# Four-tile dots, one more halving sum, a new order of gathers at the end and fewer address checks in a hard-max attention kernel

## The chip, the cores and the metric

One core of one Trainium2 chip. The metric is device time in microseconds (us) of one execution, lower is better, given as the median of several runs. A profile is one execution; its span is about 2 us shorter than the device time. PE is the matmul engine, PEld its weight loads, DVE the vector engine, ACT the scalar engine, POOL the engine that issues the gathers, SP the engine that issues most stores.

## The reference

```python
# q, k, v: (4, 4096, 128) float32
logits = np.matmul(q, k.transpose(0, 2, 1))
best = np.argmax(logits, axis=-1)
return v[b_idx, best, :].astype(np.float32)
```

Each query row gets the one value row whose key has the largest dot product with it.

## The kernel before

The 16384 query rows are 128 tiles of 128 rows. Keys are taken in groups of four. For each tile, PE computes combinations of the four keys' logits in 16 bits, ACT takes absolute values (A) and a rectified copy (E), and DVE folds everything into one score per group (`W`, line 260) and takes the best eight groups (`MAX8`, line 264). That is the main loop. Behind it runs a refinement: POOL gathers the three key differences of the best group (`kg`, "group gather"), DVE multiplies them with the query and sums (the "dots"), picks the winner (`win`), POOL gathers its value row (`vr`, "value gather") and SP stores it. Rows too close to call are flagged and done again exactly, for the first half of the tiles in mid-kernel and for the second half at the end; the end gathers their three key groups (`FK`), their queries (`FQ`) and their values (`FV`), and scatters the rows to the output.

The dots, in groups of `m` tiles (a generator; each `yield` lets the main loop go on):

```python
    def dots(c, x, m):
        ...
        for i in range(0, m, h):                       # h = min(m, 2)
            nc.vector.tensor_tensor(out=prod[:, i:i + h], in0=kg[...], in1=natq[...], op=OP.mult)
            yield gap
        nc.vector.tensor_tensor(out=p1, in0=prod[:, :, :, 0:64], in1=prod[:, :, :, 64:128], op=OP.add)
        yield gap
        nc.vector.tensor_tensor(out=p2, in0=p1[:, :, :, 0:32], in1=p1[:, :, :, 32:64], op=OP.add)
        yield "dve",
        nc.vector.tensor_reduce(out=d[:, x - c0:x - c0 + m, 1:4], in_=p2, axis=AX_X, op=OP.add)
```

What POOL issues in iteration `it`: first group gathers (`near_q`), then flagged-row gathers (`fast`), then as many value gathers (`late_q`) as the rate leaves room for:

```python
        while near_q and (n < 1 + behind or near_q[0] in marks):
            ...
        rate = 2.42 if it < 72 else 2.5 if it < 104 else 2.55 if it < 120 else 3.0
        room[0] = min(room[0] + rate - busy, 3.0) - n
        for i in range(2):
            if room[0] >= 1 and late_q:
                take_late(1)
                room[0] -= 1
```

The end, once DVE has the flagged keys' addresses `gb`:

```python
        late(LATE)                                     # 6 value gathers
        get(FK[:, 0, :], k_flat, gb[:, 0:1], B * Sk)
        get(FQ, q_flat, row, P * T)
        for r in (1, 2):
            get(FK[:, r, :], k_flat, gb[:, r:r + 1], B * Sk)
        ...
        late(1 << 20)                                  # all value gathers that are left
        ...
        get(FV, v_flat, win, B * Sk)                   # then the scatter
```

## Time and profile before

| | before |
|---|---|
| device time, median | 444.38 us (444.23 to 445.06, 4 runs) |
| span of the profiled run | 443.07 us |
| busy share of the span | PE 86%, DVE 92%, ACT 85%, POOL 70% |
| tiles 16 to 71 (stage A) | 164.40 us |
| tiles 72 to 107 (stage B) | 120.36 us |
| tiles 108 to the fold of tile 127 (stage C) | 61.11 us |
| fold of tile 127 to the final scatter | 29.88 us |

The stages are cut at the start of a tile's fold (DVE W). An engine's busy share is an average over stages with different limits.

### The profile page before, as it was taken

The numbers are of one execution on the slowest core, as the hardware profiler recorded it, in microseconds if no ns is written. First come the engines' busy times: TensorE is split into PE (matmuls) and PEld (weight loads), VectorE is DVE, ScalarE is ACT, GpSimd is POOL, SyncE is SP. The second block draws the span as 40 slices with busy tenths as digits, with TensorE's granted clock in tenths as the row PEclk, the third lists the DMA queues.
The fourth block names the chain that finished last, engine by engine and source line by source line (L and its number), as shares of the span: only waits on it lengthen the run. The fifth ranks groups of instructions, "written<-read, shape, count | busy, mean of one in ns | idle before, by whom it ended". The sixth has DMA issues, their size and how long they took to land.

```text
span 443.1 us, 6303 instructions
## 1 busy us (share of the span) xinstructions
PE 379.9 (86%) x1830; PEld 168.3 (38%) x1830; DVE 408.3 (92%) x770; ACT 377.0 (85%) x437; POOL 310.8 (70%) x335
## 2 busy tenths in 40 slices
PE   8999999999999999999998889899988999893010
PEld 4444444444444444444443333343333333331000
DVE  2688999999999999999999999999999999999861
ACT  2999999999999999999998889889988999983000
POOL 8423456777767887777778776777777777756773
PEclk9999999999999999999999999999999999998555
DMA  7944989473316999843346884354322333322341
GB/s 129 198 100 81 149 143 142 102 134 86 107 49 141 167 151 165 167 111 93 83 109 133 159 153 102 88 133 113 86 83 86 85 92 104 90 75 80 91 149 53
DMA packets 52869, 50.55 MB, mean 114 GB/s; under 512 B 34136, under 2 KB 40890, under 8 KB 52832
## 3 DMA queue, kind: packets, MB, share of 16 engines
q0 software_dynamic: 19072, 33.87, 39.0%
q1 hardware_dynamic: 33760, 16.26, 15.1%
q8 instruction: 14, 0.23, 0.2%
q14 instruction: 23, 0.19, 0.1%
HBM read 40.05 MB, written 14.55 MB: 123 GB/s over the span
## 4 chain that ended last, share of the span: by engine, by line
ACT 30%; issue 23%; DVE 17%; PE 11%; POOL 10%; DMA 7%; POOLq 0%; ACTq 0%; DVEq 0%; SPq 0%
ACT A L234 25%; DVE TOP L264 5%; POOL vr L341 5%; DVE W L260 5%; ACT E L247 5%; POOL kg L282 5%; PE psn L225 4%; DMA kg<-k,cand 4%; PE psn L244 3%; PE pd L225 3%; DVE prod L300 2%; DMA natk<-in_k_dram 2%; DVE p L305 1%; DMA FK<-in_k_dram,gb_e 1%; DMA vr<-in_v_dram,win_w 1%
## 5 line engine op out<-in xcount | busy, mean ns | idle before, releaser
L234 ACT ACTIVATE A<-pd 128x1024 f16<-128x1024 f32 x256 | 259.8, 1041 | 12.7 <-PE pd L225 11.6
L282 POOL DMA_INDIRECT kg<-k,cand x126 | 126.1, 1001 | 80.0 <-DVE cand L276 47.1
L260 DVE SCALAR_TENSOR_TENSOR W<-psn,E 128x1024 int16<-128x1024 f32 x128 | 168.0, 1312 | 7.4 <-ACT E L247 5.3
L225 PE MATMUL psn<-kT,qT 128*128 128x512 f16 x512 | 151.9, 378 | 12.7 <-ACT A L234 5.8
L225 PE MATMUL pd<-kT,qT 128*128 128x512 f16 x512 | 151.8, 378 | 9.6 <-ACT A L234 8.7
L341 POOL DMA_INDIRECT vr<-in_v_dram,win x126 | 130.8, 1038 | 39.5 <-issue 35.3
L264 DVE MAX8 TOP<-W 128x8 f32<-128x1024 f32 x128 | 157.9, 1234 | 0.0
L225 PEld LDWEIGHTS <-qT 128*128 128x128 f16 x1024 | 98.0, 97 | 154.8 <-issue 65.3
L244 PE MATMUL psn<-A,identh 128*128 128x512 f16 x512 | 152.1, 378 | 0.0
L247 ACT ACTIVATE E<-psn 128x1024 int16<-128x1024 f32 x128 | 132.2, 1033 | 3.6 <-PE psn L244 2.9
L244 PEld LDWEIGHTS <-identh 128*128 128x128 f16 x512 | 49.6, 97 | 60.8
L300 DVE TENSOR_TENSOR prod<-kg,natq 128x768 f16<-128x768 f16 x63 | 35.5, 563 | 4.5 <-DMA kg<-k,cand 4.4
L205 ACT ACTIVATE kT<-uk 128x256 f16<-128x256 f32 x48 | 20.1, 420 | 1.6 <-PE uk L202 1.6
L305 DVE TENSOR_TENSOR p<-prod 128x384 f16<-128x384 f16 (+1 forms) x45 | 19.7, 438 | 0.1
L310 DVE TENSOR_REDUCE D<-p 128x6 f32<-128x192 f16 (+1 forms) x45 | 19.1, 426 | 0.1
L201 PE MATMUL uk<-identh,natk 128*128 128x128 f16 x96 | 15.8, 218 | 0.0
L484 PE MATMUL fp_e<-n_e,tri 128*128 128x1 f32 x2 | 0.6, 362 | 16.6 <-DVE n_e L482 16.6
L308 DVE TENSOR_TENSOR p<-p 128x192 f16<-128x192 f16 (+1 forms) x45 | 13.3, 298 | 0.1
L202 PEld LDWEIGHTS <-natk 128*128 128x128 f16 x96 | 9.3, 97 | 7.0 <-issue 4.4
L66 POOL DMA_DIRECT2D natk<-in_k_dram x19 | 11.3, 601 | 0.8 <-POOLq L890 0.8
L201 PEld LDWEIGHTS <-natk 128*128 128x128 f16 x96 | 9.4, 98 | 5.6
L69 POOL DMA_DIRECT2D natq<-in_q_dram x15 | 9.1, 609 | 0.0
(152 smaller groups left out, 143.3 us busy)
## 6 DMA issues: line engine op xcount, KB each, us to landing
out_dram<-vr SPq DMA_DIRECT2D x31, 256.0 KB, 2.2
natq<-in_q_dram POOLq DMA_DIRECT2D x12, 256.0 KB, 5.2
natk<-in_k_dram POOLq DMA_DIRECT2D x10, 256.0 KB, 7.1
k<-kd SPq DMA_DIRECT2D x18, 128.0 KB, 3.4
k<-natk POOLq DMA_DIRECT2D x6, 384.0 KB, 8.3
kg<-k,cand POOLq DMA_INDIRECT x126, 3.0
vr<-in_v_dram,win POOLq DMA_INDIRECT x126, 2.6
natk<-in_k_dram POOLq DMA_DIRECT2D x8, 128.0 KB, 6.2
```

The lines of the kernel that those rows point to most:

```text
L201: nc.tensor.matmul(out=o, lhsT=natk[b % 2][:, h, 4 * m + x, :], rhs=identh, start=True, stop=False)
L205: nc.scalar.activation(out=kT[b % 2][:, c:c + 256], in_=ps, func=AF.Copy)
L225: nc.tensor.matmul(out=ps[:, n * 512:(n + 1) * 512], lhsT=qT[b % 2][:, qt * P:(qt + 1) * P], rhs=kT[b % 2][:, u * 1024 + n * 512:u * 1024 ...
L234: nc.scalar.activation(out=A, in_=ps, func=AF.Abs)
L244: nc.tensor.matmul(out=ps[:, n * 512:(n + 1) * 512], lhsT=identh, rhs=A[:, n * 512:(n + 1) * 512], start=False, stop=True)
L247: nc.scalar.activation(out=E, in_=ps, func=AF.Relu, scale=QSCALE)
L260: nc.vector.scalar_tensor_tensor(out=W_t[t % NW].bitcast(I16)[:, 1::2], in0=ps, scalar=QSCALE, in1=E, op0=OP.mult, op1=OP.max)
L264: nc.vector.max(out=TOP[:, t, :], in_=W_t[t % NW].bitcast(FP32))
L282: near_q.append(lambda j=j: nc.gpsimd.indirect_dma_start(out=kg[:, j].rearrange("p f d -> p (f d)"), out_offset=None, in_=k16[t0 // NQT], ...
L300: nc.vector.tensor_tensor(out=prod[:, i:i + h], in0=kg[:, i:i + h], in1=natq[b % 2][:, x + i - b * NQT:x + i + h - b * NQT, :].unsqueeze(2 ...
L305: nc.vector.tensor_tensor(out=p1, in0=prod[:, :, :, 0:64], in1=prod[:, :, :, 64:128], op=OP.add)
L341: late_q.append(lambda j=j: nc.gpsimd.indirect_dma_start(out=vr[:, j, :], out_offset=None, in_=v_flat, in_offset=IOA(ap=win[:, i + j:i + j ...
```

## The change

Its intent: less DVE work for the dots of tiles 72 to 107, a cheaper last reduce, group gathers that reach DVE in time, and an earlier start of the flagged rows at the end. The diff is whole; the line of `cuts` gives the same list as before.

```diff
-LATE = 6
+LATE = 4
@@ dots
         yield "dve",
+        if m == 4:
+            p3 = rp.tile([P, 4, 3, 16], FP16, tag="p3", name=f"p3_{x}")
+            nc.vector.tensor_tensor(out=p3, in0=p2[:, :, :, 0:16], in1=p2[:, :, :, 16:32], op=OP.add)
+            p2 = p3
+            yield "dve",
@@ put_values
+        edge = dict(bounds_check=B * Sk - 1, oob_is_err=False) if chunks[c][1] > T - NQT else {}
         for j in range(m):
             late_q.append(lambda j=j: nc.gpsimd.indirect_dma_start(out=vr[:, j, :], out_offset=None, in_=v_flat,
-                                                                   in_offset=IOA(ap=win[:, i + j:i + j + 1], axis=0),
-                                                                   bounds_check=B * Sk - 1, oob_is_err=False))
+                                                                   in_offset=IOA(ap=win[:, i + j:i + j + 1], axis=0), **edge))
@@
-    cuts = list(range(0, T - 32 + 1, 8)) + list(range(T - 28, T - 3, 4)) + [T - 2, T]
+    cuts = list(range(0, 96 + 1, 8)) + list(range(96 + 4, T - 3, 4)) + [T - 2, T]
@@ issue
-        while near_q and (n < 1 + behind or near_q[0] in marks):
+        while near_q and (n < 1 + behind or near_q[0] in marks or it >= T - 1):
-        rate = 2.42 if it < 72 else 2.5 if it < 104 else 2.55 if it < 120 else 3.0
+        rate = 2.42 if it < 72 else 2.5 if it < 100 else 2.42
-            if room[0] >= 1 and late_q:
+            if room[0] >= 1 and late_q and it < T - 1:
@@ gathers
-            m = 4 if t1 <= T - 56 else 2
+            m = 4 if t1 <= 108 else 2
```

## The prediction

> **What bounds the kernel now.** I read the page first, then the windows by stage, then the waits, the groups by form, and last the timeline of the end. The page's first part shows no engine that is plainly free:
>
> ```profile
> PE 379.9 (86%) x1830; PEld 168.3 (38%) x1830; DVE 408.3 (92%) x770; ACT 377.0 (85%) x437; POOL 310.8 (70%) x335
> ```
>
> So it has to be split by stage. I cut at the starts of the fold (DVE W L260) of tiles 16, 72, 108 and 127. Columns of the windows view: length, then busy time of PE, PEld, DVE, ACT, POOL with instruction counts, granted clock, DMA share, GB/s.
>
> ```profile
> 63.14:227.53 164.39, 160.98 (x791) 72.23 (x790) 164.22 (x234) 163.93 (x199) 121.07 (x122) 1.00 0.63 120
> 227.53:347.90 120.37, 106.07 (x493) 45.87 (x492) 118.20 (x261) 107.55 (x122) 91.48 (x90) 1.00 0.49 113
> 347.90:409.00 61.10, 51.14 (x213) 20.30 (x211) 59.55 (x114) 51.24 (x53) 43.37 (x44) 0.97 0.32 90
> 409.00:443.10 34.10, 2.06 (x10) 1.57 (x10) 18.98 (x106) 0.00 (x0) 21.37 (x21) 0.50 0.34 97
> ```
>
> Stage A (tiles 16 to 71, four-tile dots already) takes 164.39/56 = 2.936 us a tile, DVE and ACT both full. Stage B (72 to 107, two-tile dots and the flagged rows of the first half) takes 120.37/36 = 3.344 with DVE full and ACT at 89%: DVE-bound. Stage C (108 to 127) is DVE-bound too. Stage D, the tail, has no engine full; POOL is busy 21.37 of 34.10 us, but each gather there starts about 1.30 us after the one before (below), so POOL's queue is in fact continuous.
>
> Durations overlap: in the timeline the next DVE instruction starts before the last has ended. What a DVE instruction costs a full engine is start to start. For back-to-back instructions the timeline gives 1.19 us for the fold W, 1.14 for MAX8, and for the dots:
>
> ```profile
> 123.35 0.37 DVE L308 TENSOR_TENSOR p<-p 128x384 f16<-128x384 f16 x1
> 123.61 1.25 DVE L264 MAX8 TOP<-W 128x8 f32<-128x1024 f32 x1
> 124.75 0.56 DVE L310 TENSOR_REDUCE D<-p 128x12 f32<-128x384 f16 x1
> 125.20 0.18 DVE L276 TENSOR_SCALAR cand<-TOP 128x4 uint32<-128x4 uint32 x1
> ...
> 343.22 0.24 DVE L308 TENSOR_TENSOR p<-p 128x192 f16<-128x192 f16 x1
> 343.39 1.21 DVE L264 MAX8 TOP<-W 128x8 f32<-128x1024 f32 x1
> ```
>
> That is 0.26 for a sum of 384 outputs, 0.17 for 192, 0.45 for a reduce of 384 inputs; by the same reading 0.25 for a reduce of 192, 0.465 for a product (768), 0.46 and 0.27 for the first sum (768 and 384), 0.07 for the candidates. Check: stage A per tile = 1.19 + 1.14 + (2*0.465 + 0.46 + 0.26 + 0.45 + 0.07)/4 = 2.33 + 0.54 = 2.87, plus five picks of about 0.086 per eight tiles (0.054) = 2.925, against 2.936 measured. The method holds.
>
> **What the Trainium skill says.** "VectorE: DVE Perf Modes", section "The perf-mode tier table", has a 16-bit tensor_tensor at two elements a cycle and tensor_reduce at one. The trace agrees: 384 to 192 saves 0.09 us in the sum and 0.20 in the reduce. So a halving sum before a reduce pays only while what it removes exceeds its fixed part. "Perfetto Trace Analysis", section "Optimizing Scalar/DVE Operations", says that profiled latency is about twice the overhead because the write acknowledgement overlaps the next instruction: that is why I use start to start (0.17) and not duration (0.25). The same page, "DMA Instruction — SWDGE (GPSIMD)", says that the profiled end is the end of descriptor generation, not of the transfer; here a group gather is 1.00 us on POOL and 3.0 to landing. No page states what an address check costs; the trace does, below.
>
> **The change part by part.**
> (1) Third halving sum in four-tile dots: adds 0.17, turns the reduce from 0.45 into 0.25. Net 0.03 us per group. In stage A half the time ACT is at its own floor (two A at 0.904, one E at 0.915, half a transposed unit of 0.264: 2.855 a tile), so perhaps 0.3 us in all.
> (2) Four-tile dots for tiles 72 to 107, which had pairs. A pair costs 0.465 + 0.27 + 0.17 + 0.25 + 0.07 = 1.22, or 0.61 a tile; a new group of four 2*0.465 + 0.46 + 0.26 + 0.17 + 0.25 + 0.07 = 2.14, or 0.535. 36 tiles x 0.075 = 2.7 us, all on the bound engine. By durations it would read 4.3; I take the start-to-start figure. The list of chunks is only rewritten: the same cuts.
> (3) Fewer value gathers per tile (2.42 instead of 2.5, 2.55, 3.0), so POOL runs less far behind and group gathers come earlier. DVE's waits for them:
>
> ```profile
> DVE prod L300 <- DMA kg<-k,cand: 4.4, 8, 1.1
> ```
>
> Of the 4.4 us, some 2.1 lie in B, 1.4 in C, 0.9 in the tail. A four-tile group also has a whole tile more for its second half. I expect 1.6 back in B, 1.0 in C.
> (4) The check on 96 value gathers: 96 register moves fewer on POOL in the instruction order. POOL duration with and without it, on gathers of equal size:
>
> ```profile
> L512 POOL DMA_INDIRECT FK<-in_k_dram,gb_e x3 | 3.0, 1000 | 0.9 <-issue 0.6 <-DVE F_e L523 0.3
> L564 POOL DMA_INDIRECT xk<-in_k_dram,xc x2 | 1.9, 956 | 0.6 <-DVE p L308 0.6
> ```
>
> 44 ns x 96 = 4 us of POOL time, but in A to C POOL has slack and the tail keeps the check: nothing directly on the path.
> (5) The end. Before, DVE waits in the tail for the last group gather, which stands behind two value gathers; then six values stand before the flagged keys (FK).
>
> ```profile
> 411.90 1.29 POOL L282 DMA_INDIRECT kg<-k,cand  x1 [0.31 <-issue]
> ...
> 414.81 0.56 DVE L300 TENSOR_TENSOR prod<-kg,natq 128x768 f16<-128x768 f16 x1 [0.93 <-DMA kg<-k,cand]
> ...
> 425.19 1.00 POOL L512 DMA_INDIRECT FK<-in_k_dram,gb_e  x1 [0.31 <-DVE F_e L523]
> ...
> 433.13 0.99 POOL L341 DMA_INDIRECT vr<-in_v_dram,win_w  x1 [0.30 <-issue]
> 434.95 1.00 POOL L512 DMA_INDIRECT FV<-in_v_dram,xw_fe  x1 [0.82 <-DVE xw_fe L607]
> 438.88 1.02 POOL L541 DMA_INDIRECT out_dram<-FV,rowk_e  x1 [2.94 <-DMA out_dram<-vr]
> ```
>
> Count from the last MAX8 (410.33, call it 0). The order of instructions before has, from the last pair's first group gather (-2.3) to the last value gather (+22.8), 20 gathers without a gap. After: 21 (the slower rate leaves one value more), in the order kg kg xk v xk, 4 v, FK FQ FK FK, 8 v. The group gathers come at -2.3 and -1.0, four values end near +9. FK needs gb_e, which DVE had at +12.3; without the wait for kg about +11.3, so FK starts at +11.6 instead of +14.9. POOL then idles 2.3 us. FK, FQ, FK, FK and eight values at 1.304 put the last value at 11.6 + 11*1.304 = +26.0 instead of +22.8. From there to the scatter is 5.75 us (landing, store, wait) as before. FV could follow right behind it. So the final scatter, which waits for the last store, moves **3.2 us later** counted from the last MAX8: FK earlier helps nobody, because the bound of the tail is the count of POOL's gathers.
>
> Sum: A -0.3; B -2.7 - 1.6 = -4.3; C -1.0; tail +3.2. Together -2.4: 444.4 becomes 442.0.
>
> **Rivals.** (i) The tail turns out neutral or a gain: then the total is near 438.8, or 437 if FK earlier shortens it. For: the tail was evidently rearranged to start FK earlier, and FV before stood 0.82 us idle for DVE. Against: the store of the last values already decides the scatter, 2.94 us after FV. (ii) DVE's gain in B is swallowed by late group gathers: POOL needs per tile two gathers at 1.27 and 1.26, loads and flags, near 2.98 of the new 3.2, so it has little slack, and bursts of four gathers could make new waits. Then 444 to 446. Against: stage A runs four-tile groups with no DVE idle at all. (iii) Durations rather than starts are what DVE saves (4.3 instead of 2.7): 440.4. (iv) Faster by over 2% needs -8.9 us, which means every gain at its highest and no loss in the tail; I see no part that large.
>
> **Range and chances.** I centre on 441.8, a little under the sum, since a gain in the tail is likelier than a worse loss. 438.5 to 444.5 covers rivals (i) mostly, (iii), and a weak form of (ii). Faster by over 2%: 0.04; within 2%: 0.95; slower: 0.01.
>
> **What would show it.** Right: the sum p3 near 0.25 us long with a reduce near 0.34; tiles 72 to 107 in about 116 us; prod waiting for kg under 2 us in all; value gathers shorter by 40 ns where unchecked; FK about 11.6 us after the last MAX8 with a POOL gap before it; the scatter about 31.7 us after that MAX8 (28.55 before), still waiting for a store. Wrong: a DVE wait for kg in stage B larger than before (rival ii); POOL full before FK and the scatter at 29 us or less after the last MAX8 (rival i).

## More of the kernel before

In the flagged rows of the first half, two small matmuls add up DVE's counts `n2`; PE executes in program order, so it stands there until DVE has the counts:

```python
        nc.vector.tensor_reduce(out=n2[:, 2:3], in_=F4, axis=AX_X, op=OP.add)
        yield "dve", 0.17
        yield "wait", 1                                # one iteration later:
        ...
        nc.tensor.matmul(out=ps[:, 0:1], lhsT=tri, rhs=n2[:, 0:1], start=True, stop=True)
        nc.tensor.matmul(out=ps[:, 512:515], lhsT=ones, rhs=n2, start=True, stop=True)
```

## The result, and the profile after

The changed kernel takes 444.18 us (median of 4 runs, 443.86 to 444.89) against 444.38 before. The ratio is 0.9995 with a 95% interval of 0.9977 to 1.0012: no difference. (Ratios here are the mean time of one kernel's fast runs over that of the other's of the same rounds, so not quite the ratio of the medians quoted.) The profiled span fell from 443.07 to 442.41 us. I had forecast 2.4 us less.

The first part of the page of the changed kernel, which answers to the first line shown of before:

```profile
PE 380.9 (86%) x1830; PEld 168.7 (38%) x1830; DVE 405.4 (92%) x761; ACT 375.5 (85%) x437; POOL 307.3 (69%) x335
```

It looks like no change at all: DVE has 9 instructions and 3 us of busy time less, its share is the same. The windows by stage, with the same columns and the same tiles as before, show that two large changes cancel:

```profile
63.47:227.59 164.12, 161.26 (x792) 72.48 (x791) 163.88 (x249) 164.12 (x199) 120.27 (x122) 1.00 0.60 121
227.59:343.15 115.56, 106.18 (x491) 45.74 (x490) 113.94 (x229) 105.84 (x122) 85.26 (x88) 0.99 0.52 116
343.15:405.12 61.97, 51.37 (x215) 20.52 (x212) 61.46 (x123) 51.29 (x54) 46.20 (x46) 0.98 0.31 86
405.12:442.40 37.28, 2.18 (x10) 1.63 (x10) 18.77 (x106) 0.00 (x0) 21.89 (x22) 0.50 0.34 98
```

Stage A gives 0.28 us, stage B 4.80; stage C takes 0.86 back, and the stretch from the last fold to the end takes 3.2 (34.07 before from the fold at 409.00, 37.29 now). The first fold also starts 0.35 us later (16.71 against 16.36), before anything the change touches; over all nine undisturbed traces it lies between 16.36 and 16.74, so this is noise. Together -0.28 - 4.80 + 0.86 + 3.22 + 0.35 = -0.65, which is the difference of the spans.

These are single executions, and the one of before was a long one: 444.98 us, 0.6 over its median. The trace of e2_end_alone (below), which differs from the kernel before only in what is issued from the last iteration on, is a second look at the old loop: stage A 164.42, B 119.37, C 61.22. Against it stage B gives 3.81 us and not 4.80, C takes 0.75, and the sum is about -0.1, near the medians' -0.2. Most of the 1 us between the two looks at stage B is the wait for group gathers: 2.1 us there in the one, 1.3 in the other.

Look at the granted clock in stage B: 0.99, where it was 1.00. That is the trace of something the forecast had not seen.

**The waits.** Of the kernel before (engine, line and releaser; us in total, times, longest):

```profile
DVE W L260 <- PE psn L244: 1.6, 3, 0.7
...
PE fp L389 <- DVE n L384: 0.9, 1, 0.9
```

Of the changed kernel:

```profile
DVE W L260 <- PE psn L244: 2.9, 4, 1.3
...
PE fp L394 <- DVE n L389: 1.7, 1, 1.7
...
DVE prod L300 <- DMA kg<-k,cand: 0.2, 1, 0.2
```

The waits for group gathers, 4.4 us before, are down to 0.2 (which part of the change did that, the dots alone and the old rates below tell). But there is a fourth wait of the fold for PE, 1.3 us long, and PE's wait at the flag matmuls has grown. The timeline there (start, length, engine, line, operation, and in brackets the idle time before it and its releaser):

```profile
242.63 0.35 PE L393 MATMUL fp<-n,tri 128*128 128x1 f32 x2 [1.22 <-DVE n L385]
...
244.65 0.38 PE L394 MATMUL fp<-n,ones 128*128 128x3 f32 x2 [1.67 <-DVE n L389]
...
246.39 1.06 PE L244 MATMUL psn<-A,identh 128*128 128x512 f16 x2
...
249.87 1.31 DVE L260 SCALAR_TENSOR_TENSOR W<-psn,E 128x1024 int16<-128x1024 f32 x1 [1.27 <-PE psn L244]
```

PE stands twice in its own order at the flag matmuls, because DVE starts the last count at 244.40 us, where it was 242.29 before. The program has moved it: it stood ahead of the MAX8 of tile 76, and now it stands behind it (what moved it is shown with e6_no_p3 below):

```profile
243.26 1.22 DVE L264 MAX8 TOP<-W 128x8 f32<-128x1024 f32 x1
244.40 0.20 DVE L389 TENSOR_REDUCE n<-F 128x1 f32<-128x64 f32 x1
```

After that the same pair of matmuls that takes 0.59 us elsewhere takes 1.06, and the fold waits 1.27. The window of those slow matmuls:

```profile
245.95:249.35 3.40, 3.40 (x9) 1.18 (x8) 2.61 (x9) 2.74 (x3) 2.79 (x4) 0.50 1.31 193
```

The granted clock was 0.50 for 3.4 us, and 1.00 before and after. The Trainium skill, "TensorE: Matmul & The Clock Gate", section "What's actually happening", describes this: a monitor looks at PE's activity in windows of 3413 ns that run freely, and a window of idleness halves the clock. The traces agree on the windows: the half clock lasted 3.413 us, and in the clock records of all nine undisturbed traces every step lies a whole number of 3.413 us after the first step. They differ on the idleness: in the 3.41 us just before the drop PE was busy for 1.6 us, nearly half of the time.

**The dots.** The new sum and its reduce in the groups by form (busy us, mean ns of one):

```profile
L315 DVE TENSOR_REDUCE D<-p 128x12 f32<-128x192 f16 x27 | 9.3, 344 | 0.0
L312 DVE TENSOR_TENSOR p<-p 128x192 f16<-128x192 f16 x27 | 6.7, 246 | 0.0
```

246 and 344 ns long, as forecast (0.25 and 0.34).

**The check.** Value gathers of stage A, from the view of the tile `win`, first before, then after (min, median and max of the duration in ns; first and last start):

```profile
L341 POOL DMA_INDIRECT vr<-in_v_dram,win x53: 993/1002/1417, 73.8 to 226.2; - x53
```

```profile
L347 POOL DMA_INDIRECT vr<-in_v_dram,win x53: 940/950/1422, 75.9 to 226.1; - x53
```

The check is worth 52 ns each, a little over the forecast 44.

**The tail.** POOL in the timeline of the changed kernel; the last MAX8 starts at 406.45:

```profile
414.40 0.99 POOL L347 DMA_INDIRECT vr<-in_v_dram,win  x1 [0.30 <-issue]
417.96 1.05 POOL L517 DMA_INDIRECT FK<-in_k_dram,gb_e  x1 [2.56 <-DVE row_e L514]
...
432.33 1.00 POOL L347 DMA_INDIRECT vr<-in_v_dram,win_w  x1 [0.30 <-issue]
433.63 1.00 POOL L517 DMA_INDIRECT FV<-in_v_dram,xw_fe  x1 [0.30 <-issue]
438.22 1.02 POOL L546 DMA_INDIRECT out_dram<-FV,rowk_e  x1 [3.59 <-DMA out_dram<-vr]
```

FK starts 11.51 us after the last MAX8 (14.86 before), with POOL idle for 2.56 us ahead of it; the last value gather 25.88 us after it (22.80 before), and the scatter, still waiting for a store, 31.77 (28.55 before). Counted in the same way, DVE's flagged winners are done 2.7 us earlier than before, and nothing uses it.

### The profile page after: what moved, and what is told of

Same layout as the page of the kernel before. It is cut to its first block, busy times and chain, and to the rows that moved or that the text cites. A ratio compares the mean times of both kernels' runs of the same rounds, so it can differ in the third digit from the quotient of the medians.

```text
span 442.4 us, 6191 instructions
## 1 busy us (share of the span) xinstructions
PE 380.9 (86%) x1830; PEld 168.7 (38%) x1830; DVE 405.4 (92%) x761; ACT 375.5 (85%) x437; POOL 307.3 (69%) x335
## 4 chain that ended last, share of the span: by engine, by line
ACT 29%; DVE 23%; PE 20%; issue 18%; DMA 5%; POOL 3%; POOLq 0%; ACTq 0%; DVEq 0%; SPq 0%
ACT A L234 25%; DVE TOP L264 9%; PE psn L225 7%; PE pd L225 6%; PE psn L244 6%; DVE W L260 6%; ACT E L247 4%; POOL vr L347 2%; DVE prod L300 2%; DMA natk<-in_k_dram 2%; DMA vr<-in_v_dram,win 1%; DVE p L305 1%; DVE p L308 1%; DMA kg<-k,cand 1%; POOL kg L282 1%
## 5 line engine op out<-in xcount | busy, mean ns | idle before, releaser
L347 POOL DMA_INDIRECT vr<-in_v_dram,win x126 | 127.9, 1015 | 44.8 <-issue 34.1
L305 DVE TENSOR_TENSOR p<-prod 128x768 f16<-128x768 f16 (+1 forms) x36 | 18.1, 502 | 0.1
L315 DVE TENSOR_REDUCE D<-p 128x12 f32<-128x192 f16 (+1 forms) x36 | 12.3, 342 | 0.1
L308 DVE TENSOR_TENSOR p<-p 128x384 f16<-128x384 f16 (+1 forms) x36 | 11.7, 326 | 0.1
```

The costliest lines, as they stand in the source:

```text
L347: late_q.append(lambda j=j: nc.gpsimd.indirect_dma_start(out=vr[:, j, :], out_offset=None, in_=v_flat, in_offset=IOA(ap=win[:, i + j:i + j ...
```

## The experiments

My theory after the result: the change saves some 4 us in the main loop, and the new order of the end returns 3.2 of them, because POOL's count of gathers bounds the end; a further 1.3 us are lost to the half clock after PE's pause. Rivals: the tail is bound by FK and FV; the loss in the tail comes from the slower rate alone; the fold's wait at 249 us is made up later.

Eighteen runs of eight kernels were made. Four fell on one quiet chip, three on a second, where the kernel before took 444.42 and 444.17 us (medians of 11 runs each). The other eleven fell on four chips on which every kernel, the one before too, took 511 to 554 us: there PE stands for some us at a time with no releaser that the trace shows. No time of those is used. All eighteen results were correct.

### Six values ahead of FK in the changed kernel (e1_late6)

```diff
-LATE = 4
+LATE = 6
```

> The changed kernel with six value gathers instead of four ahead of the flagged keys. My theory (tail bound by the count of gathers on POOL, which stands idle 2.56 us before FK in the changed kernel): the idle closes, FK starts within 0.3 us of where it did (11.5 us after the start of the last MAX8), the last value gather and the final scatter come about 2.6 us earlier (29.2 us after that MAX8 instead of 31.8), time about 441.6 us. Rival (the tail is bound by FK, the exact dots and FV): no change or later, 444 us or more.

Measured: 442.34 us (441.38 to 442.92, 6 runs), ratio to before 0.9949 (0.9932 to 0.9965). POOL in the tail; the last MAX8 starts at 405.95:

```profile
418.27 1.07 POOL L517 DMA_INDIRECT FK<-in_k_dram,gb_e  x1 [0.30 <-DVE XD L574]
...
436.00 1.02 POOL L546 DMA_INDIRECT out_dram<-FV,rowk_e  x1 [3.52 <-DMA out_dram<-vr]
```

The gap before FK is closed, and though FK comes 0.8 us later than in the changed kernel (12.33 after the last MAX8 instead of 11.51), the scatter comes 1.7 us earlier (30.06 instead of 31.77). The gain is smaller than the 2.6 forecast, since the six values end after DVE is ready. A later FK and an earlier end: the tail is bound by the count of gathers, not by FK. The rival falls.

### The new end alone (e2_end_alone)

```diff
 (kernel before)
-LATE = 6
+LATE = 4
-        while near_q and (n < 1 + behind or near_q[0] in marks):
+        while near_q and (n < 1 + behind or near_q[0] in marks or it >= T - 1):
-            if room[0] >= 1 and late_q:
+            if room[0] >= 1 and late_q and it < T - 1:
```

> The kernel before with only the new end: group gathers first and no value gather in the last iteration, four values ahead of FK. My theory: stages A to C as before (last fold within 0.5 us of before); in the tail FK comes about 3.3 us earlier, POOL idles about 2.3 us before it, and the final scatter comes about 1.9 us later than before (30.5 us after the start of the last MAX8, against 28.55): 446.2 us. Rival (the end is a gain in itself and the loss is the slower rate): 443 us or less.

Measured: 446.28 us (445.75 to 446.88), ratio 1.0040 (1.0024 to 1.0055). The tail; the last MAX8 starts at 409.79:

```profile
421.31 1.05 POOL L512 DMA_INDIRECT FK<-in_k_dram,gb_e  x1 [2.56 <-DVE row_e L509]
...
440.21 1.02 POOL L541 DMA_INDIRECT out_dram<-FV,rowk_e  x1 [3.46 <-DMA out_dram<-vr]
```

FK 11.52 us after that MAX8, a gap of 2.56, the scatter at 30.42: as forecast. (The last fold, counted from the first, comes 0.9 us earlier than in the trace of before, where I had allowed 0.5: the fewer waits in stage B told above.) The new end by itself costs time, with the old rates: 1.9 of the 3.2 us in the tail. The rest is the one value gather more that the slower rate leaves (e5d_old_rate below), so the slower rate alone is not the cause either.

### The dots alone (e3_dots_alone, and again as e3b_dots_alone)

```diff
 (kernel before)
+        if m == 4:
+            p3 = ...                                   # as in the change
-            m = 4 if t1 <= T - 56 else 2
+            m = 4 if t1 <= 108 else 2
```

> The kernel before with only the four-tile dots up to tile 108 and the third sum; rates, checks and end as before. My theory: the last fold 3 to 4 us earlier, the tail as before (scatter 28.5 us after the last MAX8), so 440.5 to 441.5 us: better than the changed kernel, which gives the gain back in the tail. Rival (without the slower rate and the unchecked gathers the group gathers come late): over 2.5 us of DVE waits for kg and 443 us or more.

> The dots alone again, on the same chip as the same kernel with later flag matmuls. My theory: the runs fall into two groups about 1.2 us apart (440.5 and 441.7), by whether PE's pause near 243 us covers a whole window of its clock; the median 0.5 to 1.2 us over the kernel with later matmuls. Rival: no difference. On a disturbed chip nothing follows.

Measured: 441.69 us (440.51 to 443.37), ratio 0.9938 (0.9917 to 0.9959), on the first quiet chip, and 442.28 (441.55 to 442.96), ratio 0.9961 (0.9949 to 0.9973), on the second. Both are a little over the forecast. This small part of the change beats the whole by about 2 us. The tail is as before (scatter 28.66 and 28.74 us after the last MAX8). Waits for group gathers are 2.3 and 2.5 us in the two traces, none of it in stage B, where before had 2.1: the four-tile groups alone, at the old rates, took those away. The rest, in stage C and the tail, is what the other parts of the change remove (0.2 is left), and it does not help.

The two traces differ in one thing. In both, PE stands 1.2 and 1.7 us at the flag matmuls. In the second the clock then falls to half, and stage B is 115.50 us. In the first it does not:

```profile
246.00:249.40 3.40, 3.40 (x17) 1.49 (x16) 3.36 (x9) 3.40 (x5) 2.73 (x3) 1.00 1.25 194
```

17 matmuls where the changed kernel had 9; the fold's long wait is missing, and stage B is 114.10 us. So it is the half clock that costs the time (1.40 us of stage B here), not the pause itself, and whether the same pause halves the clock differs from run to run. That fits the skill's freely running windows, and the traces show it: counted in steps of 3.413 us from the clock's first step, the pause of the first trace is split over two windows, in which PE was busy for 1.8 and 2.15 us; in the second one window, with 1.64 us, holds most of it. In the nine undisturbed traces each such window at full clock in which PE was busy (as the profile models it) for 1.70 us or less was followed by the half clock, and none with 1.77 or more.

### Flag matmuls one iteration later in the changed kernel (e4_flag_later)

```diff
-        yield "wait", 1
+        yield "wait", 2
         ps = pp.tile([P, 1024], FP32, tag="u", name=f"fp_{t0}")
```

> The changed kernel with the matmuls of the flagged rows of the first half placed one iteration later in PE's order. My theory (the new DVE wait of 1.27 us at tile 79 is PE standing in order at those matmuls for the DVE counts n): PE's waits for n fall from 2.9 us to under 0.5, the DVE wait for psn near 249 us goes away, the last fold comes 1 to 1.3 us earlier. One value gather more is left for the tail in its order, so the end gives 1.3 us back: 443.5 to 444.5 in time. Rival (that wait is made up later, since DVE is not what sets the stage): the last fold does not move.

Measured: 444.48 us (444.21 to 444.98), ratio 1.0000 (0.9985 to 1.0015). PE's waits for the counts are gone from the list, the fold's waits for psn are back at 1.6 us, and the last fold comes 1.39 us earlier, counted from the first fold. The scatter is 33.08 us after the last MAX8, 1.3 later than in the changed kernel, for the one value gather more. Both halves of the forecast hold; the pause did cost time, and the later matmuls moved a value gather into the tail.

### Flag matmuls later with the dots alone (e8e_dots_flag, beside e3b_dots_alone)

The same edit on the dots alone. Runs e8_dots_flag, e8b_dots_flag, e8c_dots_flag and e8d_dots_flag of this kernel fell on disturbed chips (medians 523.77, 539.50, 544.43 and 519.73 us); nothing follows from their times.

> The kernel before with the four-tile dots to tile 108, the third sum, and the matmuls of the flagged rows one iteration later in PE's order; rates, checks and end as before. My theory: PE never pauses a whole clock window near 243 us, so no run has the half clock there: all runs at a mean granted clock of 0.955 or more, spread under 1 us, median 440.4 us (the dots alone had 440.5 in the two runs without the drop and 441.7 to 443.4 with it). Rival (the scatter of the dots alone has another cause): median 441.5 with the same two groups of runs.

> The dots alone with the flag matmuls one iteration later, again, since the first call fell on a chip where every kernel (the one before too) ran at 520 to 530 us with stalls of PE. Expected as then: if the chip is undisturbed, no half clock near 243 us in any run, all runs within 1 us, median 440.4. Rival: 441.5 and two groups of runs as in the dots alone.

> The dots alone with the flag matmuls one iteration later, a third time, since the two calls before fell on two other chips on which every kernel (the one before too) ran at 520 to 545 us with stalls of PE. On an undisturbed chip: no half clock near 243 us, all runs within 1 us of each other at a mean clock of 0.955 or more, median 440.4 us. Rival: 441.5 and two groups of runs as in the dots alone. On a disturbed chip nothing follows.

> The dots alone with the flag matmuls one iteration later, a fourth time (three chips were disturbed). On an undisturbed chip: no half clock near 243 us, all runs within 1 us of each other at a mean clock of 0.955 or more, median 440.4 us. Rival: 441.5 and two groups of runs as in the dots alone. On a disturbed chip nothing follows.

> The dots alone with the flag matmuls one iteration later, a last time. On an undisturbed chip: no half clock near 243 us, all runs within 1 us, median 440.4 us. Rival: as the dots alone, 441.5 and two groups of runs. On a disturbed chip nothing follows.

Measured on the quiet chip: 442.15 us (441.73 to 443.06, 5 runs), ratio 0.9967 (0.9954 to 0.9979). Windows of stages B and C, first of the dots alone, then with later flag matmuls:

```profile
227.55:343.05 115.50, 106.16 (x491) 45.74 (x490) 113.88 (x228) 105.81 (x122) 87.17 (x88) 0.99 0.51 115
343.05:406.22 63.17, 51.39 (x215) 20.52 (x212) 61.51 (x122) 51.31 (x54) 47.18 (x47) 0.97 0.30 90
```

```profile
227.42:341.69 114.27, 104.45 (x488) 45.19 (x487) 113.86 (x229) 105.58 (x121) 85.05 (x86) 1.00 0.51 116
341.69:405.85 64.16, 52.10 (x217) 20.80 (x215) 61.50 (x122) 51.87 (x54) 48.13 (x48) 0.98 0.30 90
```

Stage B is 1.23 us shorter, with the clock at 1.00, as the clock theory says; all five runs have a mean clock of 0.957 or more, the six of the dots alone beside them 0.950 to 0.955. But the times missed. The median is 442.15 and not 440.4 us, the runs spread over 1.3 us and not under 1, and the dots alone, spread over 1.4, do not fall into two groups and are only 0.13 us slower: of their forecasts the rival "no difference" holds. So the scatter of the runs has a cause beside the half clock, which stays open. Stage C is 0.99 us longer in this trace, and the waits say why:

```profile
DVE prod L300 <- DMA kg<-k,cand: 3.5, 3, 1.3
```

Against 2.5 us in the dots alone. That DVE comes earlier does not explain it: the first trace of the dots alone, without the half clock, has as short a stage B (114.10 us), takes 63.1 us in stage C, and keeps its gain to the end (440.55 us). What differs is POOL's order: with the later flag matmuls two value gathers move from stage B to stage C (36 and 27, counted by their starts, against 38 and 25), where POOL is behind at the old rates. In the changed kernel the same edit moved one into the tail (e4). This fits both losses, but was not tested by itself.

### The old rates in the changed kernel (e5d_old_rate)

```diff
-        rate = 2.42 if it < 72 else 2.5 if it < 100 else 2.42
+        rate = 2.42 if it < 72 else 2.5 if it < 104 else 2.55 if it < 120 else 3.0
```

Runs e5_old_rate, e5b_old_rate and e5c_old_rate fell on disturbed chips (520.25, 536.06 and 524.64 us).

> The changed kernel with the rates of value gathers of the kernel before. My theory (the slower rate removes DVE's waits for group gathers but leaves one value more for the tail): waits for kg return, 1.5 to 2.5 us in stage C as in the dots alone; 12 instead of 13 values are left from the last pair on, so the scatter comes 1.3 us earlier after the last MAX8 (30.4 instead of 31.8). Net within 0.7 us of the changed kernel, 443.5 to 444.5. Rival (group gathers first at the end make the slower rate needless): no kg wait over 0.5 us and 442.8 or less.

> The changed kernel with the old rates, again on an undisturbed chip. Expected as then: waits for kg of 1.5 to 2.5 us in stage C, scatter 30.5 us after the last MAX8 (the disturbed run had 30.51), total 443.5 to 444.5. Rival: no kg wait over 0.5 us and 442.8 or less.

> The changed kernel with the old rates, a third time. On an undisturbed chip: waits for kg of 1.5 to 2.5 us in stage C, scatter 30.5 us after the last MAX8 (30.4 to 30.5 in the disturbed runs), total 443.5 to 444.5. Rival: no kg wait over 0.5 us and 442.8 or less. On a disturbed chip nothing follows.

> The changed kernel with the old rates, a last time. On an undisturbed chip: waits for kg of 1.5 to 2.5 us in stage C, scatter 30.5 us after the last MAX8, total 443.5 to 444.5. Rival: no kg wait over 0.5 us and 442.8 or less. On a disturbed chip nothing follows.

Measured on the quiet chip: 444.22 us (443.98 to 445.06, 5 runs), ratio 1.0013 (1.0000 to 1.0026). One wait for a group gather of 1.7 us is back in stage C, which is 63.27 us instead of 61.97; the scatter comes 30.54 us after the last MAX8 instead of 31.77. The slower rate trades a wait in the loop for a gather in the tail, at par. Group gathers first in the last iteration do not replace it.

### Without the third sum, and without the checks: not settled in time

e6_no_p3 and e6b_no_p3 take the third sum out of the changed kernel; e9_dots_flag_nocheck and e9b_dots_flag_nocheck take the 96 checks off the dots with later flag matmuls. All four fell on disturbed chips (520.80, 531.44, 529.75 and 543.18 us), so what either part does to the time by itself stays open. The order of DVE's instructions, though, is the program's, on any chip. Both traces without the third sum, four-tile dots and all, have the last count ahead of the MAX8 of tile 76 again, as before (e6_no_p3; its times are those of a disturbed chip):

```profile
288.16 0.22 DVE L384 TENSOR_REDUCE n<-F 128x1 f32<-128x64 f32 x1
...
289.02 1.23 DVE L264 MAX8 TOP<-W 128x8 f32<-128x1024 f32 x1
```

So it is the third sum, not the four-tile dots, that pushes the counts back and makes PE pause. That stage B would be shorter by the pause's cost without it was not measured.

> The changed kernel without the third halving sum. My reckoning by start to start (0.17 + 0.25 against 0.45): 0.03 us a group, 27 groups, so stage A 0.3 us longer and the rest 0.3 us longer, 444.5 to 445. Rival by durations (0.25 + 0.34 against 0.56): it would be 0.8 us shorter, 443.4. It also changes the order in which DVE does the counts of the flagged rows, so the pause of PE near 243 us and the drop of its clock may be gone: if so, stage B is 1.2 us shorter and the total 443.3; the wait of W for psn tells which.

> The changed kernel without the third sum, again on an undisturbed chip. Expected as then: by start to start 0.3 us longer in stage A and 0.3 in the rest, 444.5 to 445; by durations 443.4; and if the pause of PE near 243 us goes with the order, stage B 1.2 us shorter and the total near 443.3.

> The same as the kernel with dots and later flag matmuls, with the address check taken off the 96 value gathers of the first three batches. My theory: POOL has slack in stages A and B, so the time is within 0.7 us of that kernel. Rival: 40 ns off each value gather brings the group gathers earlier where POOL is behind; then DVE's waits for kg in stage C fall from 2.4 us to about 1 and the time by about 1 us.

> Dots alone with later flag matmuls and without the check on 96 value gathers, again on an undisturbed chip. Expected as then: within 0.7 us of the same kernel with the check. Rival: kg waits in stage C down from 2.4 us to about 1 and 1 us less in time.

What the quiet traces do show of the third sum is stage A, where it is nearly all that differs on DVE: 164.40 and 164.42 us in the two traces without it, 164.07 to 164.15 in seven with it. That is the 0.3 us forecast, for 14 groups.

## Why the prediction was right or wrong

- **What bounds it, and the method of start to start: right.** Stages A and B behaved as DVE-bound. DVE's work from tile 72 to the last fold, which is the length of B and C less DVE's idle time there, fell from 181.47 - 3.71 = 177.76 to 177.53 - 2.13 = 175.40 us, by 2.4 where I had 2.7. By durations it would have been 4.3.
- **Part 1, the third sum: right in its own cost, 0.28 us in stage A against 0.3; but here is the step that failed.** I counted it as "net 0.03 us per group" on DVE and asked nothing about what stands behind it in DVE's order. It pushes the flag counts from before a MAX8 to behind it, PE pauses in its own order for them, its clock halves, and the fold waits 1.27 us.
- **Part 2, four-tile dots: right in sum, not in place.** B fell by 4.8 us (3.8 against the second trace of the old loop) instead of 4.3, and C rose by 0.9 instead of falling by 1.0, because the later group pushes two products, one sum and one pick of five instructions over the border: counted by their starts, DVE has 32 instructions fewer in B and 8 more in C. That B alone came near its forecast is luck: the new wait and this shift largely offset each other.
- **Part 3, waits for group gathers: right in direction, too small, and half wrong in its cause.** I gave 2.6 us back of 3.5 in B and C; 3.4 came. The slower rate did not do it in stage B: the four-tile groups did, which I had named in half a sentence (no such wait there in the dots alone, at the old rates). The slower rate removes some 1.5 us in stage C (1.7 with the old rates in e5d, 0.2 without) and pays 1.2 for it in the tail.
- **Part 4, the check: right.** It is real on POOL (52 ns each), and no wait that set the path was seen to change with it. Its effect on the time was not isolated.
- **Part 5, the end: right within 0.3 us.** FK at 11.51 (forecast 11.6) after the last MAX8, a gap on POOL of 2.56 (2.3), the last value gather at 25.88 (26.0), the scatter 3.2 us later (3.2). Rival (i) falls; e1 and e2 show it from both sides.
- **The sum: this failed.** "Together -2.4" had no term for a new wait in stage B. I had named one rival there, late group gathers, and looked at POOL and kg only. For B and C together I had -5.3 us, and -3.9 came (-3.1 against the second trace of the old loop). The 1.4 between are the new wait of W for PE, 1.27, another 0.35 because DVE's work fell by 2.35 and not 2.7, and 0.5 of small waits, less the 0.8 that the waits for group gathers gave back beyond the forecast. e4 and the two traces of the dots alone show the wait, the orders with and without the third sum show where it comes from.
- **The range held, and the likeliest class came**, but the forecast gain was not there: the ratio's interval includes one.

What can be had from the change is the dots alone, with the old end: 441.69 and 442.28 us on two chips, 0.4 to 0.6% under the kernel before. The changed kernel with six values ahead of FK comes to the same, 442.34. No kernel tried was faster by more than the 0.6%. Not tried: the dots alone without the third sum.

## What to carry to other kernels

Where an in-order queue sets the end, count what is left in it: starting the urgent work earlier by moving other items behind it makes the end later if the queue idles meanwhile and the moved items are the ones waited for. When instructions of one engine are regrouped, or one is added, look at every engine that waits for it in program order, small side matmuls included: here a pause of PE that held up no fold at the full clock cost stage B 1.4 us when the clock fell after it. An edit meant for one engine can reorder another's queue: the dots with later flag matmuls gained 1.2 us in one stage, where two value gathers left it, and lost 1.0 in the next, where they arrived.

## What the Trainium skill lacked or had wrong

- "TensorE: Matmul & The Clock Gate" warns of PE idle gaps over about 3 us between bursts of matmuls (section "Why this matters for your kernels"); elsewhere it tells of drops from many short pauses, without a measure. Here the longest single gap was 1.67 us, with another of 1.22 before it, and the clock fell to 0.50 for 3.41 us, which cost stage B 1.1 to 1.4 us. What told the runs apart was PE's busy time in a 3.413 us window: 1.70 us or less halved the clock, 1.77 or more did not. The same pause, split over two windows, left the clock at 1.00.
- No page has the cost of the address check of an indirect gather: 1002 ns with it, 950 without, at the median of 53 gathers each.
- No page that I found gives the pace of indirect gathers from one queue: about 1.30 us from start to start for checked ones, of which 0.30 is between instructions.
- "VectorE: DVE Perf Modes" tells to minimise the number of DVE operations; it states no break-even for one more halving sum before a reduce. Here, at 384 inputs, 14 more operations left stage A 0.3 us shorter: barely worth it.
